# Trainium2, one core: expert products collected by half features, memory splits spread over the convolution, GpSimd emptied in the second block, the norm folded into cos and sin

## The chip, the core and the metric

The kernel runs on one core of a Trainium2 chip. A core has a matrix engine (PE, with its weight loads shown as PEld), three engines for elementwise work (DVE, ACT, POOL) and a queue of DMA issues on SP. Each engine takes its instructions in the order in which the program was scheduled, and waits on semaphores for the others. The metric is device time of one execution in microseconds, lower is better.

## The reference

256 tokens of width 1024 pass a first block (modulated norms, retention and differential attention, then a mixture of 16384 single-neuron experts) and a second block of two layers. Cut to what the change touches:

```
x = x + mod[:, 5] * peer_ffn(h2, ...)              # end of the first block
# second block, layer 0                               (rms_norm before each h)
b_gate, c_gate, u = split(h @ conv_w_in, 3)
x = x + (b_gate * conv3(c_gate * u)) @ conv_w_out   # 3 taps along the tokens
x = x + mem_cross_attention(h, mem_n, ...)          # keys and values of 256 memory tokens
x = x + swiglu(h)
# layer 1
k, v = split(rms_norm(x, kv_norm) @ w_kv, 2);  k = apply_partial_rope(k, cos, sin)
q = apply_partial_rope(h @ moba_w_q, cos, sin)
x = x + causal_softmax(q k^T * 128**-0.5) v @ moba_w_o
x = x + mem_cross_attention(...);  x = x + swiglu(h);  out = rms_norm(x, g)
```

## The kernel before

**Layout and products.** Activations lie as [128 features, chunk k of 8, 256 tokens]. A product of a 128x1024 weight block with an activation is `block`: the raw block is loaded by DMA (three buffers, `raw`), ACT rounds it to `whi`, DVE or POOL subtracts to `wlo` (`split_w`, L121, two `wlo` buffers), and PE does 24 products of 128x128 by 128x256: eight chunks k each of whi·xh, wlo·xh and whi·xl (`mm3`, L143). With `late=True` the 24 run chunk by chunk, so that the first block can begin before all of x is there. The activation's own halves come from `gain_chunk`: `hh` on ACT, `hl` on DVE (L269, L270).

**Order.** A scheduler orders each engine's instructions when the program is built. By hand come two things. `PLACES` names the points (`at(...)`) where steps of a *filler* are put: one step is one 24-product block of the keys and values of the second memory attention (tiles `fill`, `hmh`, `hml`, `memk1`, `memv1`), which depends on nothing near it. And `lo_plan` and the argument `lo` say which engine makes a block's `wlo`; `FILL_LO = 'p'` puts that of the filler on POOL.

**The seam between the blocks.** Experts go in 128 chunks; chunk products of 128x512 (L948) add into four banks `acc[th][dh]` (token half, feature half). The last two chunks are done for token half 0, then 1; `collect(th)` copies four quarters out of PSUM (L956), transposes eight 128x128 tiles on PE (L961) and adds each into x with the gate (L964).

**Convolution** (`conv_mixer`). For each of eight output chunks m, PE does the blocks of c_gate, u (tile `o`) and b_gate (tile `b`). The norm's r is needed only afterwards: squares of x are summed in `track` (ACT squares, `self.adder` adds, L225), one product with ones makes the sum (`aux`), and `rstd` makes r (`nry`). `gate` then works off chunk m: cu = o·r (DVE), z (POOL), first tap (DVE), two taps (DVE), y·r (POOL), ct = b·y (DVE, L1246, reads PSUM), ch (ACT), cl (DVE). Chunk 0 is gated only when chunk 1 has been computed, so `b` of chunk 0 holds its PSUM bank until `ct` of chunk 0 is made. At m = 1, `hook()` loads the first memory attention's keys and values from DRAM (tile `kvt`, two buffers) and splits them: `memk0h`, `memv0h` on ACT, `memk0l`, `memv0l` on POOL (L1086).

**Moba layer.** w_v, then eight heads of w_k and of moba_wq. `plain` takes each out of PSUM with scale and r (`qkt`, L1373); `rope_out` shuffles (DVE), multiplies with cos (POOL, L384) and with sin (DVE, L385) and adds (DVE, L386).

Of the kernel before, what the change touches and what calls it, by code (L numbers as in the profile page):

```python
# [25 lines left out]
P = 128  # L26
# [14 lines left out]
PLACES = {0: 1, 3: 1, 5: 2, 6: 1, 10: 1, 12: 1, 's': 2, 'h': 4, 'g': 10, 'n': 1, ('g', 0): 1, 'v': 4, ('d', 1): 1, ('o', 0): 3, ('o', 2): 1, ('o', 3): 1, ('o', 4): 1, ('o', 5): 4, ('o', 7): 10, ('c', 1): 1, ('c', 3): 1, ('c', 5): 1, 'ce': 1, 'm0': 1, 'mq0': 1, 'me0': 1, 'f0': 1, 'b': 2, 'bk': 1, 'bq': 1, ('mh0', 2): 1, ('bh', 0): 1, ('bh', 5): 1, ('bh', 7): 1}  # L41
# [7 lines left out]
HOOK = 1  # L49
# [6 lines left out]
CADD = 'vector'  # L56
# [14 lines left out]
class Build:  # L71
    def __init__(self, ctx, tc, io):
        self.ctx, self.tc, self.nc, self.io = ctx, tc, tc.nc, io
        self.const = ctx.enter_context(tc.tile_pool(name="const", bufs=1))
        self.wpool = ctx.enter_context(tc.tile_pool(name="weights", bufs=2))
        self.psfill = ctx.enter_context(tc.tile_pool(name="psfill", bufs=1, space=PSUM))
        self.lo_turn = 0
        self.folding = []
        self.filler = self.steady = iter(())
        self.rate, self.due = RATE, 0  # L80
        self.adder = self.nc.gpsimd
        self.lo_plan = "v"
# [356 lines left out]
    def mixer(self):  # L439
        nc, io, tc = self.nc, self.io, self.tc  # L440
        with ExitStack() as ctx:
# [7 lines left out]
            with ExitStack() as c1:  # L449
# [18 lines left out]
                self.adder = nc.vector  # L468
# [235 lines left out]
    def peer(self):  # L704
        nc, io = self.nc, self.io
        with ExitStack() as ctx:
# [237 lines left out]
            def product(c, th, a, b, w):  # L944
                tsl = slice(th * P, th * P + P)
                for s, (x, wt) in enumerate(((a, w[0]), (b, w[0]), (a, w[1]))):
                    for dh in range(2):
                        nc.tensor.matmul(acc[th][:, dh], x[:, tsl], wt[:, dh * 512:dh * 512 + 512],  # L948
                                         start=c == 0 and s == 0, stop=c == NCH - 1 and s == 2)

            def collect(th):

                tsl = slice(th * P, th * P + P)
                for q in range(4):
                    e = nc.scalar.copy if th or q % 2 else nc.vector.tensor_copy
                    e(ot[:, th, q * T:(q + 1) * T], acc[th][:, q // 2, q % 2 * T:q % 2 * T + T])  # L956
                for q in range(2):
                    tr = self.psum([P, 4, P])
                    for i in range(4):
                        k = 4 * q + i  # L960
                        nc.tensor.transpose(tr[:, i], ot[:, th, k * P:(k + 1) * P], self.ident)  # L961
                    for i in range(4):
                        k = 4 * q + i
                        nc.vector.scalar_tensor_tensor(self.x[:, k, tsl], tr[:, i], gate[:, k:k + 1],  # L964
                                                       self.x[:, k, tsl], op0=OP.mult, op1=OP.add)
# [12 lines left out]
            for c, parts in ends:  # L978
                product(c, 0, *parts)
            product(ends[0][0], 1, *ends[0][1])  # L980
            collect(0)
            product(ends[1][0], 1, *ends[1][1])
            collect(1)


    def mem_kv(self, pool, mpool, l, key, value, norm=None):
# [38 lines left out]
        yield from self.natural_steps("fill", [io["mem_wv"][l, q] for q in range(8)], toks,  # L1025
                                      lambda n, i, o: value(n, o, rn), FILL_LO)
# [47 lines left out]
    def mem_load(self, pool, l):  # L1074
# [3 lines left out]
        def load():  # L1078
            for n in range(4):
                for part in range(2):  # L1080
# [5 lines left out]
                    nc.gpsimd.tensor_sub(lo, t, hi)  # L1086

        return (kT, v), load

    def mem_fill(self, pool, mpool, l):  # L1090
# [3 lines left out]
        def key(n, o, r):  # L1094
# [4 lines left out]
            nc.gpsimd.tensor_sub(lo, t, hi)  # L1099
# [125 lines left out]
    def conv_mixer(self, hook):  # L1225
        nc, io = self.nc, self.io
        with ExitStack() as ctx:
# [5 lines left out]
            def gate(m, o, b):  # L1233
                cu = pool.tile([P, 2, T], F32, name="cu", tag="cu", bufs=2)
                nc.vector.tensor_mul(cu, o, r[:, None, :].to_broadcast([P, 2, T]))
                z = pool.tile([P, T], F32, name="z", tag="z", bufs=2)
                nc.gpsimd.tensor_mul(z, cu[:, 0], cu[:, 1])
                y = pool.tile([P, T], F32, name="cy", tag="cy", bufs=2)
                nc.vector.tensor_scalar(y, z, cw[:, m, 2:3], None, op0=OP.mult)
# [4 lines left out]
                nc.gpsimd.tensor_mul(y, y, r)  # L1244
# [5 lines left out]
            self.adder = getattr(nc, CADD)  # L1250
            for k in range(KC):
                self.track(self.x[:, k], k)
            self.adder = nc.gpsimd
            for m in range(KC):
                self.at(("c", m))
                if m == HOOK:
                    hook()
                o = self.psum([P, 2, T], "sc" if m < 2 else "mm")
                for i, c in enumerate((1, 2)):
                    self.block(o[:, i], io["conv_wi"][8 * c + m], h, late=m == i == 0)  # L1260
                    if m == 1 and i == NORM1:
                        r = self.tracked_norm(pool, "nr", tables=True)
                b = self.psum([P, T])
# [78 lines left out]
    def moba(self):  # L1342
        nc, io = self.nc, self.io
        with ExitStack() as ctx:
            pool = self.pool(ctx, "moba")
            mask = self.load(pool, "causal", [P, 2, T])
            hk = self.gained(pool, self.x, G_KV)
            v = pool.tile([P, 2, 1024], F32, name="v")
# [5 lines left out]
            def value(n, i, o):  # L1354
# [3 lines left out]
                if n == 1:  # L1358
                    rn = self.by_partition(pool, r, "aux")
                waiting.append((n, o))  # L1360
# [8 lines left out]
            def plain(block, h, scale):  # L1369
                o = self.psum([P, T])  # L1370
                self.block(o, block, h)
                t = pool.tile([P, T], F32, name="qkt", tag="qkt", bufs=3)
                nc.vector.scalar_tensor_tensor(t, o, scale, r, op0=OP.mult, op1=OP.mult)  # L1373
                return t

            def rope(out, t):
                self.rope_out(pool, t, out, self.pcos, self.psin)
# [4 lines left out]
            hq = [self.placed(pool, "hq" + c, 32) for c in "hl"]  # L1382

            def query(hd):
                return plain(io["moba_wq"][hd], hq, 128.0 ** -0.5)
# [5 lines left out]
            for hd in range(KC):  # L1391
                t = plain(io["w_k"][hd], hk, 1.0)
# [3 lines left out]
                self.gain_chunk(self.x[:, hd], G_MIX + 1, hd, hq[0][:, hd], hq[1][:, hd])  # L1396
# [224 lines left out]
```

## Time and profile before

| | |
|---|---|
| median of 3 runs | 1904.57 us (1903.88 to 1911.25) |
| profiled execution | 1898.9 us, of it the span of the trace 1897.0 us |
| mean granted TensorE clock | 0.984 |
| busy: PE, DVE, ACT, POOL | 1830.2, 1324.2, 968.1, 541.2 us |
| last expert product, start | 1127.17 us into the span |
| convolution, first product to last | 1132 to 1255 us, about |
| moba layer | 1505 to 1630 us, about |
| second memory attention, second swiglu | 1633 to 1700, 1704 to 1885 us, about |

Times are microseconds from the span's start. Some 60% of the span lies ahead of the seam and is the same code in both kernels; the change acts from about 1125 us on.

### The profile page before, as it was taken

The page shows a single profiled execution, that of the slowest core. Times are in us where ns is not written, and L with a number is a line of the kernel's source. Part 1 is how long each engine was busy: PE and PEld are TensorE (multiplying, and loading weights), DVE is VectorE, ACT ScalarE, POOL GpSimd, SP SyncE. Part 2 cuts the span into 40 slices and gives each one's busy share as a digit, 9 for nine tenths or more (in the row PEclk, how much of TensorE's full clock was granted, in tenths as well). Part 3 has the DMA queues.
Part 4 walks back from the last instruction along what each step waited for, and adds up shares of the span by engine and source line. Part 5 has one row for each costly group of instructions (what it writes and reads, how often), then busy time and mean ns, then how long its engine had stood idle before and what let it go on. Part 6 is the DMA issues. An engine that isn't in the chain of part 4 may idle for free.

```text
span 1897.0 us, 34717 instructions
## 1 busy us (share of the span) xinstructions
PE 1830.2 (96%) x13488; PEld 1713.1 (90%) x13488; DVE 1324.2 (70%) x2594; ACT 968.1 (51%) x1517; POOL 541.2 (29%) x289
## 2 busy tenths in 40 slices
PE   5899999999999999999999998999999999999997
PEld 4696788999999999788888878999999998999997
DVE  8988965995556676865555568677765678766654
ACT  5645534545554444454545454455554545555543
POOL 2511115787776767100000004242000222110001
PEclk8999999999999999999999998999999999999999
DMA  7673435555444444765656565654666553545553
GB/s 265 222 244 101 133 123 169 172 194 170 163 152 157 155 160 152 251 190 190 198 190 195 192 201 168 190 165 152 197 195 195 188 177 120 167 133 183 187 188 123
DMA packets 99765, 335.13 MB, mean 177 GB/s; under 512 B 12400, under 2 KB 13456, under 8 KB 99216
## 3 DMA queue, kind: packets, MB, share of 16 engines
q1 hardware_dynamic: 98160, 330.68, 53.4%
q8 instruction: 106, 1.74, 0.4%
q10 hardware_dynamic: 1440, 2.23, 0.3%
q14 instruction: 59, 0.48, 0.1%
HBM read 329.59 MB, written 3.28 MB: 175 GB/s over the span
## 4 chain that ended last, share of the span: by engine, by line
PE 86%; DVE 8%; ACT 2%; issue 2%; DMA 1%; POOL 1%; SPq 0%; DVEq 0%; ACTq 0%; POOLq 0%
PE mm L143 53%; PE pair L948 18%; PE mm L178 4%; PE pair L885 3%; PE fill L178 1%; PE fill L143 1%; DVE wlo L121 1%; PE sc L143 1%; PE aux L143 1%; ACT whi L117 1%; DMA mraw<-w_mod 0%; PE sc L546 0%; POOL wlo L121 0%; DMA raw<-w_mod 0%; DVE macc L361 0%
## 5 line engine op out<-in xcount | busy, mean ns | idle before, releaser
L117 ACT CAST whi<-raw 128x1024 fp32r<-128x1024 f32 x564 | 591.8, 1051 | 548.8 <-PE mm L143 261.6
L121 DVE TENSOR_TENSOR wlo<-raw,whi 128x1024 fp32r<-128x1024 f32 x389 | 489.1, 1259 | 277.9 <-PE pair L948 130.7
L121 POOL TENSOR_TENSOR wlo<-raw,whi 128x1024 fp32r<-128x1024 f32 x175 | 425.2, 2431 | 276.3 <-PE mm L143 169.2
L143 PE MATMUL mm<-hh,whi 128*128 128x256 f32 (+1 forms) x1184 | 177.6, 287 | 6.5 <-DVE ct L1246 5.0
L225 POOL TENSOR_TENSOR acc<-acc,accsq 128x256 f32<-128x256 f32 x42 | 42.6, 1015 | 491.3 <-ACT accsq L223 491.3
L143 PE MATMUL mm<-hl,whi 128*128 128x256 f32 (+1 forms) x1184 | 174.4, 285 | 0.9 <-DVE hl L270 0.9
L143 PE MATMUL mm<-hh,wlo 128*128 128x256 f32 (+1 forms) x1184 | 173.5, 285 | 0.6 <-DVE wlo L121 0.6
L143 PE MATMUL mm<-h2h,whi 128*128 128x256 f32 x1152 | 166.9, 287 | 4.1 <-ACT h2h L255 4.0
L143 PEld LDWEIGHTS mm<-hh,whi 128*128 128x128 f32 x1184 | 154.4, 190 | 12.0 <-issue 7.4
L948 PE MATMUL pair<-whi,actl 128*128 128x512 f32 x512 | 159.0, 392 | 1.8 <-DVE actl L941 1.8
L948 PE MATMUL pair<-whi,acth 128*128 128x512 f32 x512 | 158.7, 391 | 0.4 <-ACT acth L940 0.4
L948 PE MATMUL pair<-wlo,acth 128*128 128x512 f32 x512 | 158.4, 391 | 0.3 <-DVE wlo L121 0.3
L143 PEld LDWEIGHTS mm<-hh,wlo 128*128 128x128 f32 x1184 | 153.4, 189 | 4.3 <-issue 1.5
L143 PEld LDWEIGHTS mm<-hl,whi 128*128 128x128 f32 x1184 | 153.5, 189 | 3.5 <-DVE hl L270 1.6
L143 PE MATMUL mm<-h2l,whi 128*128 128x256 f32 x1152 | 156.1, 278 | 0.0
L143 PE MATMUL mm<-h2h,wlo 128*128 128x256 f32 x1152 | 156.0, 278 | 0.0
L143 PEld LDWEIGHTS mm<-h2h,whi 128*128 128x128 f32 x1152 | 146.3, 191 | 5.0 <-ACT h2h L255 4.8
L143 PEld LDWEIGHTS mm<-h2l,whi 128*128 128x128 f32 x1152 | 143.1, 188 | 0.0
L143 PEld LDWEIGHTS mm<-h2h,wlo 128*128 128x128 f32 x1152 | 143.0, 188 | 0.0
L948 PEld LDWEIGHTS pair<-whi,actl 128*128 128x128 f32 x512 | 95.9, 188 | 23.1 <-DVE actl L941 3.2
L948 PEld LDWEIGHTS pair<-wlo,acth 128*128 128x128 f32 x512 | 96.6, 189 | 20.9 <-DVE wlo L121 0.7
L948 PEld LDWEIGHTS pair<-whi,acth 128*128 128x128 f32 x512 | 96.0, 188 | 20.7 <-ACT acth L940 1.0
(408 smaller groups left out, 3111.5 us busy)
## 6 DMA issues: line engine op xcount, KB each, us to landing
raw<-peer_u SPq DMA_DIRECT2D x128, 512.0 KB, 3.5
raw<-peer_v SPq DMA_DIRECT2D x128, 512.0 KB, 3.5
raw<-ffn_gu SPq DMA_DIRECT2D x88, 512.0 KB, 3.9
raw<-ffn_dn SPq DMA_DIRECT2D x44, 512.0 KB, 3.5
raw<-w_mod SPq DMA_DIRECT2D x64, 256.0 KB, 3.8
raw<-conv_wi SPq DMA_DIRECT2D x24, 512.0 KB, 3.6
raw<-mem_wk SPq DMA_DIRECT2D x16, 512.0 KB, 5.2
mraw<-w_mod SPq DMA_DIRECT2D x16, 512.0 KB, 6.2
```

The costliest lines, as they stand in the source:

```text
L117: self.hi_copy = nc.scalar.copy(hi, raw)
L121: (nc.vector if plan == "v" else nc.gpsimd).tensor_sub(lo, raw, hi)
L143: self.matmul = nc.tensor.matmul(out, a, b, start=first and j == 0, stop=last and j == 3 * n - 1)
L178: self.matmul = nc.tensor.matmul(outs[i // 2][:, i % 2], a[:, k, :], b[:, w], start=k == 0 and s == 0 and i % 2 == 0, stop=k == 7 and s == ...
L225: self.adder.tensor_add(self.acc, self.acc, self.last)
L885: nc.tensor.matmul(o[:, 2 * j + i], A[:, i], Bt[:, i], start=True, stop=True)
L948: nc.tensor.matmul(acc[th][:, dh], x[:, tsl], wt[:, dh * 512:dh * 512 + 512], start=c == 0 and s == 0, stop=c == NCH - 1 and s == 2)
```

## The change

Six edits. (1) The last two chunks' products and `collect` go by feature half dh, with th inside; each `collect(th, dh)` has one ACT copy, one DVE copy, four transposes and four additions. (2) `late` takes a number: the convolution's first block does chunks 0 to 3 in all three products, then 4 to 7. (3) `mem_load` is a generator; two of its eight steps are drawn for each m from 3 on, instead of all at m = 1, and its subtractions, those of the second memory's loads and the `wlo` of the filler are on DVE. (4) Two filler steps no longer stand at m = 1 and m = 3; they are left to the `fill(20)` ahead of the second memory attention. (5) `self.adder` is DVE in the second block, `gate` has its two POOL multiplications on DVE (z = o0·r², then z·o1, both from PSUM), and its first tap is on ACT. (6) In the moba layer r is multiplied into cos and sin once (`cosr`, `sinr`), the scale of q into its gains, and `rope` reads the product in PSUM directly with four DVE instructions.

```diff
-PLACES = {..., ('c', 1): 1, ('c', 3): 1, ('c', 5): 1, ...}
+PLACES = {..., ('c', 5): 1, ...}
-HOOK = 1
+HOOK = 3
-        self.adder = self.nc.gpsimd
+        self.adder = self.nc.vector
...
-            order.sort(key=lambda si: (si[1], si[0]))
+            order.sort(key=lambda si: (si[1] // int(late), si[0], si[1]))
...
-            def collect(th):
+            def collect(th, dh):
...
+                for q, e in zip((2 * dh, 2 * dh + 1), (nc.scalar.copy, nc.vector.tensor_copy)):
+                    e(ot[:, th, q * T:(q + 1) * T], acc[th][:, dh, q % 2 * T:q % 2 * T + T])
...
-            for c, parts in ends:
-                product(c, 0, *parts)
-            product(ends[0][0], 1, *ends[0][1])
-            collect(0)
-            product(ends[1][0], 1, *ends[1][1])
-            collect(1)
+            waiting = None
+            for dh in range(2):
+                for th in range(2):
+                    for c, parts in ends:
+                        product(c, th, *parts, halves=(dh,))
+                    if waiting:
+                        collect(*waiting)
+                    waiting = th, dh
+            collect(*waiting)
...
-                self.block(o[:, i], io["mem_wk"][l, 2 * m2 + i], hm, lo=FILL_LO, late=m2 == i == 0,
+                self.block(o[:, i], io["mem_wk"][l, 2 * m2 + i], hm, lo="v" if l else FILL_LO, late=m2 == i == 0,
...
-                    nc.gpsimd.tensor_sub(lo, t, hi)
+                    nc.vector.tensor_sub(lo, t, hi)
+                    yield
...
-                cu = pool.tile([P, 2, T], F32, name="cu", tag="cu", bufs=2)
-                nc.vector.tensor_mul(cu, o, r[:, None, :].to_broadcast([P, 2, T]))
-                nc.gpsimd.tensor_mul(z, cu[:, 0], cu[:, 1])
+                nc.vector.tensor_mul(z, o[:, 0], r2)
+                nc.vector.tensor_mul(z, o[:, 1], z)
-                nc.vector.tensor_scalar(y, z, cw[:, m, 2:3], None, op0=OP.mult)
+                nc.scalar.activation(y, z, AF.Copy, scale=cw[:, m, 2:3])
...
-                nc.gpsimd.tensor_mul(y, y, r)
+                nc.vector.tensor_mul(y, y, r)
...
-                if m == HOOK:
-                    hook()
+                if m >= HOOK:
+                    for _ in range(2):
+                        next(hook, None)
...
+                    nc.vector.tensor_mul(cosr, self.pcos, r)
+                    nc.vector.tensor_mul(sinr, self.psin, r)
...
+            def rope(out, o):
+                t = pool.tile([P, T], F32, name="roper", tag="roper", bufs=2)
+                nc.vector.stream_shuffle(t, o, [(i + 16) % 32 for i in range(32)])
+                nc.vector.tensor_mul(out, o, cosr)
+                nc.vector.tensor_mul(t, t, sinr)
+                nc.vector.tensor_add(out, out, t)
                 return out
```

How the scheduler's order moves is shown at three places; line numbers of the changed kernel are one or two lower for the same code. First DVE at the seam, before: the quarter copies out of PSUM (`slots<-pair`), two splits of convolution weights (`wlo`), the additions into x, then `hl` for the convolution.

```order
L956 COPY slots<-pair 128x256 x2
L121 TENSOR_TENSOR wlo<-raw,whi 128x1024
L964 SCALAR_TENSOR_TENSOR x<-mm,mod,x 128x128 x8
L121 TENSOR_TENSOR wlo<-raw,whi 128x1024
L964 SCALAR_TENSOR_TENSOR x<-mm,mod,x 128x128 x8
L270 SCALAR_TENSOR_TENSOR hl<-x,gains,hh 128x256 x8
L225 TENSOR_TENSOR acc<-acc,accsq 128x256
L121 TENSOR_TENSOR wlo<-raw,whi 128x1024
```

The same place on DVE in the changed kernel:

```order
L953 COPY slots<-pair 128x256 x2
L960 SCALAR_TENSOR_TENSOR x<-mm,mod,x 128x128 x8
L953 COPY slots<-pair 128x256
L120 TENSOR_TENSOR wlo<-raw,whi 128x1024
L960 SCALAR_TENSOR_TENSOR x<-mm,mod,x 128x128 x4
L953 COPY slots<-pair 128x256
L120 TENSOR_TENSOR wlo<-raw,whi 128x1024
L960 SCALAR_TENSOR_TENSOR x<-mm,mod,x 128x128 x4
L269 SCALAR_TENSOR_TENSOR hl<-x,gains,hh 128x256 x8
L224 TENSOR_TENSOR acc<-acc,accsq 128x256
L120 TENSOR_TENSOR wlo<-raw,whi 128x1024
L224 TENSOR_TENSOR acc<-acc,accsq 128x256
```

One copy and one split now stand between the last two groups of additions, and all eight `hl` still come after the last addition.

Second, POOL from the first memory split to the third gated chunk, before (in the changed kernel POOL has nothing between the last expert chunk and the final norm):

```order
L1086 TENSOR_TENSOR memk0l<-kvt,memk0h 128x512
L1086 TENSOR_TENSOR memv0l<-kvt,memv0h 128x2x256
L1237 TENSOR_TENSOR z<-cu 128x256
L1086 TENSOR_TENSOR memk0l<-kvt,memk0h 128x512
L1237 TENSOR_TENSOR z<-cu 128x256
L1086 TENSOR_TENSOR memv0l<-kvt,memv0h 128x2x256
L1244 TENSOR_TENSOR cy<-cy,nry 128x256
L121 TENSOR_TENSOR wlo<-raw,whi 128x1024
L1244 TENSOR_TENSOR cy<-cy,nry 128x256
```

And DVE of the changed kernel from the norm's last step (`nry`) to `ct` of the first two chunks:

```order
L211 SCALAR_TENSOR_TENSOR nry<-nra,nry 128x256
L120 TENSOR_TENSOR wlo<-raw,whi 128x1024
L1263 TENSOR_TENSOR r_12403<-nry 128x256
L269 SCALAR_TENSOR_TENSOR hml<-memx,gains,hmh 128x256
L1235 TENSOR_TENSOR z<-sc,r_12403 128x256 x2
L1236 TENSOR_TENSOR z<-sc,z 128x256 x2
L120 TENSOR_TENSOR wlo<-raw,whi 128x1024
L1239 SCALAR_TENSOR_TENSOR cy<-z,conv_w,cy 128x255 x2
L1241 SCALAR_TENSOR_TENSOR cy<-z,conv_w,cy 128x254 x2
L1243 TENSOR_TENSOR cy<-cy,nry 128x256 x2
L1245 TENSOR_TENSOR ct<-mm,cy 128x256 x2
```

Between the end of the `hl` and the first `ct` DVE holds seven `wlo`, four of the eight memory splits, eight additions to `acc`, seven `hml`, the norm and the gating of two chunks; the other four memory splits come after it.

Third, DVE in the moba layer where the first two filler blocks stand, before, from the rope of the last head of k to that of the second head of q:

```order
L386 TENSOR_TENSOR k<-k,roper 128x256
L1373 SCALAR_TENSOR_TENSOR qkt<-mm,nry 128x256
L383 STREAM_SHUFFLE roper<-qkt 128x256
L385 TENSOR_TENSOR roper<-roper,psin 128x256
L386 TENSOR_TENSOR q<-q,roper 128x256
L121 TENSOR_TENSOR wlo<-raw,whi 128x1024
L1373 SCALAR_TENSOR_TENSOR qkt<-mm,nry 128x256
```

The same place in the changed kernel:

```order
L1388 TENSOR_TENSOR k<-k,roper 128x256
L120 TENSOR_TENSOR wlo<-raw,whi 128x1024
L1385 STREAM_SHUFFLE roper<-mm 128x256
L1386 TENSOR_TENSOR q<-mm,cosr 128x256
L1387 TENSOR_TENSOR roper<-roper,sinr 128x256
L1388 TENSOR_TENSOR q<-q,roper 128x256
L120 TENSOR_TENSOR wlo<-raw,whi 128x1024
L1385 STREAM_SHUFFLE roper<-mm 128x256
```

Before, the `wlo` of these two filler blocks are on POOL; the first `wlo` in this piece is now that of the first filler block.

## Rows read from the trace of the kernel before

**Rows 1.** The page, part 4: shares of the chain that ended last.
```profile
PE 86%; DVE 8%; ACT 2%; issue 2%; DMA 1%; POOL 1%; SPq 0%; DVEq 0%; ACTq 0%; POOLq 0%
```

**Rows 2.** Stretches: length, busy PE, PEld, DVE, ACT, POOL (count), granted clock, DMA share.
```profile
1136.00:1166.00 30.00, 23.41 (x176) 22.63 (x175) 26.44 (x30) 17.02 (x28) 16.48 (x11) 0.89 0.61 194
1166.00:1180.00 14.00, 12.13 (x84) 12.16 (x85) 10.44 (x16) 5.23 (x7) 5.58 (x5) 0.76 0.34 107
1180.00:1255.00 75.00, 74.39 (x646) 74.02 (x646) 51.99 (x72) 37.31 (x50) 26.72 (x22) 1.00 0.59 190
```

**Rows 3.** PE from 1127 to 1174: start, length, instruction, count [idle before, releaser].
```profile
1127.17 0.62 PE L948 MATMUL pair<-wlo,acth 128*128 128x512 f32 x2
...
1132.11 0.55 PE L143 MATMUL sc<-hh,whi 128*128 128x256 f32 x1 [2.07 <-ACT hh L269]
...
1136.95 1.07 PE L143 MATMUL sc<-hh,whi 128*128 128x256 f32 x8
...
1146.79 2.07 PE L143 MATMUL sc<-hh,wlo 128*128 128x256 f32 x8 [3.27 <-DVE wlo L121]
...
1161.82 1.07 PE L143 MATMUL mm<-hl,whi 128*128 128x256 f32 x8
1167.87 2.04 PE L143 MATMUL mm<-hh,whi 128*128 128x256 f32 x8 [4.98 <-DVE ct L1246]
...
1173.08 0.28 PE L143 MATMUL fill<-hmh,whi 128*128 128x256 f32 x1
```

**Rows 4.** DVE from 1131 to 1172, columns as in the rows above.
```profile
1131.93 3.24 DVE L270 SCALAR_TENSOR_TENSOR hl<-x,gains,hh 128x256 fp32r<-128x256 f32 x8
...
1139.86 0.48 DVE L270 SCALAR_TENSOR_TENSOR hml<-memx,gains,hmh 128x256 fp32r<-128x256 f32 x1
1140.26 0.42 DVE L225 TENSOR_TENSOR acc<-acc,accsq 128x256 f32<-128x256 f32 x1
1140.60 1.52 DVE L270 SCALAR_TENSOR_TENSOR hml<-memx,gains,hmh 128x256 fp32r<-128x256 f32 x1
...
1145.53 5.65 DVE L121 TENSOR_TENSOR wlo<-raw,whi 128x1024 fp32r<-128x1024 f32 x3
...
1158.53 1.22 DVE L121 TENSOR_TENSOR wlo<-raw,whi 128x1024 fp32r<-128x1024 f32 x1
...
1167.30 0.42 DVE L1246 TENSOR_TENSOR ct<-mm,cy 128x256 f32<-128x256 f32 x1 [0.61 <-POOL cy L1244]
...
1171.17 0.68 DVE L1235 TENSOR_TENSOR cu<-mm,nry 128x512 f32<-128x512 f32 x1
```

**Rows 5.** POOL at the first memory split.
```profile
1140.26 1.58 POOL L1086 TENSOR_TENSOR memk0l<-kvt,memk0h 128x512 fp32r<-128x512 f32 x1 [370.24 <-ACT memk0h L1085]
```

**Rows 6.** PE in the moba layer, the two filler blocks that wait.
```profile
1560.04 0.38 PE L178 MATMUL fill<-wlo,hmh 128*128 128x256 f32 x1 [1.13 <-POOL wlo L121]
...
1569.55 0.55 PE L178 MATMUL fill<-whi,hmh 128*128 128x256 f32 x1 [3.23 <-DVE bsst L1123]
...
1572.43 0.28 PE L178 MATMUL fill<-whi,hml 128*128 128x256 f32 x1
```

**Rows 7.** DVE in the moba layer, an addition that ends a rope, and the filler's value.
```profile
1557.85 2.41 DVE L386 TENSOR_TENSOR k<-k,roper 128x256 f32<-128x256 f32 x1
...
1568.54 0.87 DVE L1105 SCALAR_TENSOR_TENSOR memv1l<-fill,memrn,memv1h 128x256 fp32r<-128x256 f32 x2
```

**Rows 8.** POOL in the moba layer, the filler's first split.
```profile
1557.42 2.56 POOL L121 TENSOR_TENSOR wlo<-raw,whi 128x1024 fp32r<-128x1024 f32 x1
```

**Rows 9.** Waits of PE after 1110: releaser, us in total, times, longest.
```profile
PE mm L143 <- DVE hl L270: 0.9, 3, 0.5
...
PE mm L143 <- ACT ch L1247: 0.6, 1, 0.6
```

**Rows 10.** The chain in order of time, the two longest pieces: start, us, what.
```profile
1324.95 174.11 PE mm L143 x1536
...
1704.27 180.92 PE mm L143 x1536
```

More of the change, by code (lines that the diff above doesn't have):

```diff
@@ L55 @@
 BYP = 2
-CADD = 'vector'
 MIXLO = 'v'
@@ L942, in chunk, with product @@
                 return a, b, w
-            def product(c, th, a, b, w):
+            def product(c, th, a, b, w, halves=range(2)):
                 tsl = slice(th * P, th * P + P)
                 for s, (x, wt) in enumerate(((a, w[0]), (b, w[0]), (a, w[1]))):
-                    for dh in range(2):
+                    for dh in halves:
                         nc.tensor.matmul(acc[th][:, dh], x[:, tsl], wt[:, dh * 512:dh * 512 + 512],
                                          start=c == 0 and s == 0, stop=c == NCH - 1 and s == 2)
-            def collect(th):
+            def collect(th, dh):
                 tsl = slice(th * P, th * P + P)
[L954 to L965, printed above, removed]
+                for q, e in zip((2 * dh, 2 * dh + 1), (nc.scalar.copy, nc.vector.tensor_copy)):
+                    e(ot[:, th, q * T:(q + 1) * T], acc[th][:, dh, q % 2 * T:q % 2 * T + T])
+                tr = self.psum([P, 4, P])
+                for i in range(4):
+                    k = 4 * dh + i
+                    nc.tensor.transpose(tr[:, i], ot[:, th, k * P:(k + 1) * P], self.ident)
+                for i in range(4):
+                    k = 4 * dh + i
+                    nc.vector.scalar_tensor_tensor(self.x[:, k, tsl], tr[:, i], gate[:, k:k + 1],
+                                                   self.x[:, k, tsl], op0=OP.mult, op1=OP.add)
             gate = self.mod[:, 40:48, 0]
@@ L1248, in gate @@
                 nc.vector.tensor_sub(cat[1][:, m], t, cat[0][:, m])
-            self.adder = getattr(nc, CADD)
+            self.adder = nc.vector
             for k in range(KC):
                 self.track(self.x[:, k], k)
-            self.adder = nc.gpsimd
             for m in range(KC):
                 self.at(("c", m))
-                if m == HOOK:
-                    hook()
+                if m >= HOOK:
+                    for _ in range(2):
+                        next(hook, None)
                 o = self.psum([P, 2, T], "sc" if m < 2 else "mm")
                 for i, c in enumerate((1, 2)):
-                    self.block(o[:, i], io["conv_wi"][8 * c + m], h, late=m == i == 0)
+                    self.block(o[:, i], io["conv_wi"][8 * c + m], h, late=4 if m == i == 0 else 0)
                     if m == 1 and i == NORM1:
                         r = self.tracked_norm(pool, "nr", tables=True)
+                        r2 = pool.tile([P, T], F32, name="r2")
+                        nc.vector.tensor_mul(r2, r, r)
                 b = self.psum([P, T])
@@ L1347, in moba @@
             hk = self.gained(pool, self.x, G_KV)
+            nc.vector.tensor_scalar(self.gains[:, G_MIX + 1], self.gains[:, G_MIX + 1], 128.0 ** -0.5, None,
+                                    op0=OP.mult)
+            hq = [self.placed(pool, "hq" + c, 40) for c in "hl"]
+            cosr, sinr = (pool.tile([P, T], F32, name=n) for n in ("cosr", "sinr"))
             v = pool.tile([P, 2, 1024], F32, name="v")
@@ L1359, in value @@
                     rn = self.by_partition(pool, r, "aux")
+                    nc.vector.tensor_mul(cosr, self.pcos, r)
+                    nc.vector.tensor_mul(sinr, self.psin, r)
+                for k in (2 * n, 2 * n + 1):
+                    self.gain_chunk(self.x[:, k], G_MIX + 1, k, hq[0][:, k], hq[1][:, k])
                 waiting.append((n, o))
@@ L1367, in moba, with plain @@
             self.natural("mm", [io["w_v"][q] for q in range(8)], toks, value)
-            def plain(block, h, scale):
+            def plain(block, h):
                 o = self.psum([P, T])
                 self.block(o, block, h)
[L1372 to L1377, printed above, removed]
+                return o
+            def rope(out, o):
[4 more added lines that the diff above has]
+                nc.vector.tensor_add(out, out, t)
                 return out
@@ L1381, in moba @@
             kT = pool.tile([P, KC, T], F32, name="k")
-            hq = [self.placed(pool, "hq" + c, 32) for c in "hl"]
             def query(hd):
-                return plain(io["moba_wq"][hd], hq, 128.0 ** -0.5)
+                return plain(io["moba_wq"][hd], hq)
             def turned(t):
```

12 lines of the change are left out of this document (5 added, 7 removed).

## The prediction

> **What bounds the kernel now.** I read the chain of waits first. PE holds 86% of it and DVE 8% [rows 1], so a change off PE can only pay where PE stands still or runs at the lower granted clock. Next the table of stretches after the seam. From 1180 on the convolution is full of PE: 74.39 busy of 75 us at a granted clock of 1.00. Ahead of that it is not: 23.41 of 30 us at 0.89, then 12.13 of 14 us at 0.76 [rows 2]. The timeline of PE says where. The first product of the convolution waits 2.07 us, a block in chunk 1 waits 3.27 us for a `wlo` of DVE, and the `b` block of chunk 2 waits 4.98 us for `ct` of chunk 0, which frees its PSUM bank [rows 3]. From 1167.87 to 1173.08 that block's 24 products take 5.21 us [rows 3]; at the rate of the first swiglu (174.11 us for 1536 products, 0.1133 each) they take 2.72 [rows 10]. So a wait costs about 2.5 us more than itself, the time at the lower level of the clock, 1.2 GHz instead of 2.4, that follows it.
>
> Why is DVE late there? Between 1136 and 1166 it is busy 26.44 of 30 us beside POOL's 16.48 [rows 2], but many of its instructions are stretched. `hml` takes 0.48 us, and 1.52 once it starts at 1140.60, while POOL's `memk0l` runs from 1140.26 for 1.58 [rows 4, 5]; three `wlo` take 5.65 us where three single ones take 3 x 1.22 = 3.66 [rows 4]. The moba layer shows the same: the addition at 1557.85 takes 2.41 us beside a `wlo` on POOL that runs from 1557.42 for 2.56 [rows 7, 8], where an addition of that size takes 0.42 [rows 4]. PE then waits 1.13 us for that POOL split and 3.23 us for a PSUM bank of the filler, whose reader `memv1l` stands behind the late ropes on DVE at 1568.54 [rows 6, 7].
>
> The Trainium skill ("SBUF — State Buffer", section Who interferes with whom) says that a DVE instruction with two SBUF inputs and a GpSimd instruction that reads SBUF exclude each other for a whole instruction. The rows agree: the 1.52 us `hml` ends 0.28 us after `memk0l`. The page's practical rule, that the one to issue second blocks until the first finishes, would make every POOL operation beside DVE cost its full length, and by it the gain of the convolution would lie at the upper end given below.
>
> **The change part by part.** *Seam.* Before, the last expert product ends at 1127.17 + 0.62 = 1127.79; I call this t0. The `hl` run from t0+4.14 to t0+7.38 [rows 4], and the 28 products ahead of 1136.95 are done at t0+9.16 [rows 3]. In the new order the eight `hl` still stand behind the last addition, and that behind, in turn, four additions, a copy and a split. Half of eight additions is about 1.1 us (an `hl`, 0.40 each, is a larger one), the copy 0.4 and the split 1.2, then four more additions 1.1, with hops: `hl` begins at about t0+5 and ends at t0+8.35, 1 us later. Against this the `hh` of chunks 0 to 3 are ready while the last products run, so PE needs only the last few products after the last `hl`: 28 done at t0+8.6 to t0+9.2. I take 0, with bounds of -1 and +1 us.
>
> *Convolution.* Two POOL multiplications a chunk and eight memory splits go to DVE. Their price there: the split of 128x512 has the size of `cu`, 0.68 us; the others are of 128x256, 0.42 [rows 4]. The two stretched pieces above alone give back 1.04 and 1.99 us. So DVE's work up to the first `ct`, by the new order after the last `hl`, each counted from start to next start (some 0.08 us less than its length): eight `acc` at 0.33 are 2.7 us, seven `wlo` at 1.14 are 8.0, four splits at 0.61 are 2.4, seven `hml` at 0.40 are 2.8, four steps of the norm 1.8, r2 0.35, four `z` 1.4, four taps 1.7, two multiplications by r 0.8 and `ct` 0.4: together 22.4 us, hence t0+8.35+22.4 = t0+30.7. Before, `ct` ended at 1167.30 + 0.42, t0+39.9 [rows 4]. PE meanwhile has, after its 28 products, 164 more to the same place (20 left of the first `b`, six blocks of 24): 164 x 0.1133 = 18.6 us, so it arrives at about t0+27.5 and still waits some 3 us, no longer 4.98, and the 3.27 us wait in chunk 1 and its slow time are swallowed. After the wait I leave the slow 5.21 us as it was. Gain 39.9 - 30.7 = 9.2 us. Upper bound: DVE ahead of PE, no wait and no slow time, 39.9 - 27.5 + 2.5 = 15. Lower bound: DVE also waits for ACT's first tap, for `whi` and for `wlo` buffers that PE frees; 6 us of that leaves 3. I take 9.
>
> From chunk 2 on a chunk has 72 products, 8.16 us. DVE then does three `wlo` (3.4 us), `z` twice, two taps, y·r, `ct`, `cl` (seven at about 0.4, 2.8 us), in all 6.2, with two memory splits 7.4. That lies under PE, and no gain is left there but the 0.6 us for `ch` [rows 9]. The two filler steps only move; their 48 products cost the same elsewhere.
>
> *Second layer.* `wlo` of the filler at 1.22 us on DVE costs its queue less than the 2.0 us by which a POOL split stretched the addition. In the new order the first filler's `wlo` stands ahead of the first rope of q, so the 1.13 us go; `memv1l` comes about one split and two additions behind its product, so of the 3.23 I leave 0.6; the slow time after it (13 products took 1572.43 - 1569.55 = 2.88 us until the clock came back, for 1.5 at full rate [rows 6]) goes too, 1.3. Sum 5.1; I take 4.5, bounds 2 and 5.7. If the cover of PE's queue were gone, the four rope instructions, now reading PSUM and holding the bank longer, would cost up to 0.4 each for ten heads, 4 us; PE's own 2.72 us a head hides all but the last. *Second memory attention.* Two more filler blocks stand ahead of it and cover `hl`: 0.9 us [rows 9]; I take 0.7, bounds 0 and 2. The sums on DVE instead of POOL (0.42 each, some 35) lie under PE's products: 0.
>
> **Sum.** 0 + 9.0 + 0.5 + 4.5 + 0.7 = 14.7 us. The profiled execution took 1898.9 us (1897.0 of span and 1.9 around it), 5.7 under the median; I subtract from either: 1884.2 beside the profile, 1904.6 - 14.7 = 1889.9 as a median. Bounds of the terms together: 1 lost at the seam, 3, 0, 2, 0 is 4; 1, 15, 0.6, 5.7, 2 is 24. The time is 1880 to 1901 by these.
>
> **The rivals.** A measurement of this kernel can tell about 0.5%, 9.5 us: faster is below 1895.0, slower above 1914.1.
>
> *A, forecast:* gain 10 to 20, about 1890.
>
> *B, DVE becomes the bound of the convolution's start.* For it speaks that DVE was 88% busy there [rows 2] and takes on all of POOL's work in strict order; against it, that much of these 88% is stretch. At 6 us of waits the gain is 3 + 5.7 = 8.7, no measurable change, 1896. The Trainium skill ("Perfetto Trace Analysis", section Optimizing Scalar/DVE Operations) would rather take work off a full DVE, even to GpSimd, but adds that the shared port may spoil this; the rows show that it does here.
>
> *C, the rate of PE changes with the new order.* The same 1536 products of a swiglu take 174.11 us in layer 0 and 180.92 in layer 1 [rows 10], both at granted clock 1.00, with nothing waited for: 0.1133 against 0.1178 a product. I found no cause in the rows. If the first layer (about 390 us at the faster rate) falls to the slower one, 390 x 0.04 = 15.6 us are lost and the gain is gone, 1905, no change; for the first swiglu alone 6.8, 1897. If the second swiglu rises instead, 6.8 more are won, 1883.
>
> *D, the other side: DVE above 8.16 us in every chunk of the convolution.* Each `gate` now has two round trips to ACT (first tap, `ch`) with `wlo` queued behind. Were each exposed at 2 us, a chunk would take 7.4 + 4 = 11.4 us of DVE, 3.2 above PE, over six chunks 19 us, plus about half as much in lower clock as after the waits above, 28 in all: 1890 + 28 = 1918, slower. It begins to cost at 0.8 us of exposed waiting a chunk, and makes the kernel slower by over 0.5% from about 3.5. Against it: `cl` stands after other work in the new order, and first taps come in pairs.
>
> *E, the stalls were not the bound,* and another wait (weights' DMA) takes their place: about 1901. PE is 0.99 busy right after 1180 with a DMA share of 0.59, beside 0.61 before [rows 2], which speaks against it.
>
> **Chances.** A 0.50, C upward (1878 to 1885) 0.14, B 0.12, C downward 0.12, E 0.05, D 0.07. The likeliest gives 1890; its own range is 1884 to 1895. Leaving out D and the tails of C, 1879 to 1905. Below 1895: A almost whole, C upward, a little of B and C downward, 0.66; slower is D, 0.07; the rest, 0.27, the same.
>
> **What would show it.** Right: no POOL row after the seam but the last, `hml` at 0.48 throughout, the `ct` wait at about t0+27.5 of some 3 us and none for `wlo` before it, 1.13 and 3.23 us gone in the moba layer, the convolution's last product some 9 us earlier against t0 plus the moved filler's 5.7. Wrong: `hl` ending later than t0+9, a DVE wait in every chunk, a swiglu of layer 0 near 181 us.

## The result, and the profile after

The changed kernel takes 1892.76 us (median of 16 runs, 1887.35 to 1899.19) beside 1905.54 of the kernel before (16 runs, 1897.81 to 1912.35). The ratio on record is 0.9938, 95% interval 0.9921 to 0.9954: faster by 0.62%, which is 11.8 us, between 8.8 and 15.1; the two medians lie 12.8 us apart. Forecast were 1890 us, 14.7 us faster, and a range of 1879 to 1905. Two repetitions of the changed kernel gave 0.9928 (0.9909 to 0.9947) and 0.9932 (0.9905 to 0.9958). The profiled execution took 1892.6 us, 1890.7 of it span.

What PE waits for after the seam, by the list of waits (releaser, us in total, times, longest; only those over 1 us). The 3.3 and 5.0 us of the convolution and both waits of the moba layer are gone or smaller; 2.7 us for `memv1l` are new:

```profile
PE fill L177 <- DVE memv1l L1105: 2.7, 1, 2.7
PE sc L142 <- ACT hh L268: 1.8, 1, 1.8
PE mm L142 <- DVE ct L1245: 1.7, 1, 1.7
PE mm L957 <- DVE slots L953: 1.5, 1, 1.5
```

PE at the seam and the start of the convolution, from the first of the last 24 expert products to the block after the `ct` wait (to be read beside [rows 3]):

```profile
1126.31 0.39 PE L946 MATMUL pair<-whi,acth 128*128 128x512 f32 x1
...
1133.07 0.39 PE L946 MATMUL pair<-wlo,acth 128*128 128x512 f32 x1
...
1138.38 0.71 PE L142 MATMUL sc<-hh,whi 128*128 128x256 f32 x4 [1.82 <-ACT hh L268]
...
1143.29 1.07 PE L142 MATMUL sc<-hh,whi 128*128 128x256 f32 x8
...
1161.80 1.10 PE L142 MATMUL mm<-hl,whi 128*128 128x256 f32 x8
1164.60 1.15 PE L142 MATMUL mm<-hh,whi 128*128 128x256 f32 x8 [1.70 <-DVE ct L1245]
...
1167.41 1.07 PE L142 MATMUL mm<-hh,whi 128*128 128x256 f32 x8
```

t0, the end of the last expert product, is 1133.07 + 0.39 = 1133.46. The 28th product is done at 1143.29, t0+9.8 (before t0+9.2); the waiting block starts at t0+31.1 (before 1167.87, t0+40.1); and its 24 products take 1167.41 - 1164.60 = 2.81 us at a granted clock of 1.00, not 5.21. DVE over the same stretch:

```profile
1138.15 3.24 DVE L269 SCALAR_TENSOR_TENSOR hl<-x,gains,hh 128x256 fp32r<-128x256 f32 x8
...
1144.34 0.68 DVE L1085 TENSOR_TENSOR memk0l<-kvt,memk0h 128x512 fp32r<-128x512 f32 x1
...
1149.60 0.48 DVE L269 SCALAR_TENSOR_TENSOR hml<-memx,gains,hmh 128x256 fp32r<-128x256 f32 x1
...
1164.04 0.75 DVE L1245 TENSOR_TENSOR ct<-mm,cy 128x256 f32<-128x256 f32 x2
```

`hml` takes 0.48 us and a memory split 0.68. The first `ct` ends at 1164.04 + 0.41 = 1164.45, t0+31.0; forecast was t0+30.7. By stretches (busy PE, PEld, DVE, ACT, POOL, granted clock, as in [rows 2]), POOL has nothing left, DVE is busy 0.98 of the time until the waiting block and 0.96 in the 15 us after it, with PE full at the clock of 1.00:

```profile
1143.29:1164.60 21.31, 19.61 (x168) 19.38 (x167) 20.79 (x41) 18.10 (x32) 0.00 (x0) 1.00 0.80 256
1164.60:1180.00 15.40, 15.40 (x136) 15.40 (x137) 14.85 (x26) 8.27 (x12) 0.00 (x0) 1.00 0.63 206
```

**The stages of all profiles.** One execution's total mixes the change with the rate of PE (next section), so I compare stages between rows that both kernels have: from the first of the last 24 expert products to the first swiglu's 1536 products, these products, and from their end to those of the second swiglu. For before that is 1324.95 - 1121.09, 174.11, and 1704.27 - 1499.06 [rows 10], with this row of before:

```profile
1121.09 0.61 PE L948 MATMUL pair<-whi,acth 128*128 128x512 f32 x2
```

All stages are in us. A star marks kernels in which 48 filler products are done after the first stage instead of in it (5.7 us, two blocks of 2.86).

| kernel | seam to swiglu 1 | swiglu 1 | to swiglu 2 | ratio to before, 95% interval |
|---|---|---|---|---|
| before | 203.9 | 174.1 | 205.2 | |
| before, again | 203.3 | 180.9 | 205.4 | |
| changed * | 185.3 | 180.9 | 205.5 | 0.9938, 0.9921 to 0.9954 |
| changed, again * | 185.0 | 180.9 | 208.3 | 0.9928, 0.9909 to 0.9947 |
| changed, third * | 185.3 | 180.9 | 206.0 | 0.9932, 0.9905 to 0.9958 |
| splits on DVE alone | 197.1 | 180.9 | 205.3 | 0.9959, 0.9937 to 0.9981 |
| spreading alone | 199.6 | 180.9 | 205.1 | 0.9992, 0.9975 to 1.0009 |
| splits, spreading and moba | 199.6 | 180.9 | 200.0 | 0.9916, 0.9886 to 0.9945 |
| moba alone | 204.0 | 180.9 | 198.9 | 0.9987, 0.9975 to 0.9999 |
| filler's splits on DVE alone | 203.0 | 180.9 | 201.2 | 0.9963, 0.9945 to 0.9982 |
| changed, seam as before * | 186.3 | 180.9 | 206.4 | 0.9947, 0.9926 to 0.9967 |
| changed, gating on POOL * | 189.4 | 180.9 | 207.0 | 0.9956, 0.9937 to 0.9976 |
| changed, filler in the heads * | 188.9 | 180.9 | 204.0 | 0.9922, 0.9898 to 0.9946 |
| the same again * | 187.1 | 180.9 | 204.4 | 0.9917, 0.9892 to 0.9942 |

By the means of the profiles, and with the 5.7 us set right, the change gives 203.6 - (185.2 + 5.7) = 12.7 us in the first stage and 205.3 - (206.6 - 5.7) = 4.4 in the second, 17.1 in all. PE has two rates inside these stages too. Counted by the distance from one product's start to the next (0.113 or 0.118 us), 366 and 445 products of the first stage are at the slower rate in before's two profiles, and 376, 378 and 373 in the changed kernel's; in the second stage 883 and 635 beside 608, 806 and 762. In the means that is some 0.3 of the 17.1 us; between single profiles it can be 1 to 2 us.

### The profile page after: what moved, and what is told of

It reads as the page before. It is cut to its first block, busy times and chain, and to the rows that moved or that the text cites. A ratio compares the mean times of both kernels' runs of the same rounds, so it can differ in the third digit from the quotient of the medians.

```text
span 1890.7 us, 34567 instructions
## 1 busy us (share of the span) xinstructions
PE 1829.8 (97%) x13488; PEld 1715.8 (91%) x13488; DVE 1337.7 (71%) x2678; ACT 970.1 (51%) x1523; POOL 413.1 (22%) x187
## 4 chain that ended last, share of the span: by engine, by line
PE 87%; DVE 7%; ACT 2%; DMA 2%; issue 1%; POOL 0%; SPq 0%; DVEq 0%; ACTq 0%; POOLq 0%
PE mm L142 55%; PE pair L946 17%; PE mm L177 4%; PE pair L883 3%; PE fill L177 2%; PE fill L142 2%; PE sc L142 1%; DMA raw<-peer_v 1%; DVE wlo L120 1%; PE aux L142 1%; DMA kvt<-kv 0%; DMA raw<-w_mod 0%; DVE mlo L120 0%; POOL wlo L120 0%; ACT whi L116 0%
## 5 line engine op out<-in xcount | busy, mean ns | idle before, releaser
L120 DVE TENSOR_TENSOR wlo<-raw,whi 128x1024 fp32r<-128x1024 f32 x405 | 496.6, 1227 | 261.5 <-PE pair L946 130.7
L120 POOL TENSOR_TENSOR wlo<-raw,whi 128x1024 fp32r<-128x1024 f32 x159 | 386.1, 2429 | 228.1 <-PE mm L142 157.9
```

What stands on the lines that cost most here:

```text
L120: (nc.vector if plan == "v" else nc.gpsimd).tensor_sub(lo, raw, hi)
```

## The experiments

**The rates of PE.** Both kernels once more, unedited, and the changed one a third time.

> The changed kernel once more. Theory A (the two rates of PE, 0.1133 and 0.1178 us a product of 128x256, fall out anew in each execution): the first swiglu's 1536 products, 180.9 us in the first profile, can come out at 174 as well, and the 767 products of the experts' query stage, which no edit touches (90.3 us there, 87.0 before), change too. Theory B (the change's new order sets the rate): the first swiglu stays at 181 and the query stage at 90. Both: the time about 1892 and the stretch from the end of the expert products to the third chunk's b block of the convolution the same as in the first profile within 0.5 us.

> The kernel before once more, for its rates. Theory A: the first swiglu (174.1 us in the first profile) or the second (180.9) or the query stage (87.0) comes out otherwise. Theory B: 174.1, 180.9 and 87.0 again. Both: the waits of PE in the convolution as before, 3.3 us for the weight split and 5.0 us for ct.

The chain's longest pieces, first of the changed kernel, then of its repetition, then of before's repetition and of the kernel with the spreading alone (start, us, what):

```profile
359.55 90.34 PE mm L142 x767
...
1311.64 180.91 PE mm L142 x1536
...
1698.01 180.92 PE mm L142 x1536
```

```profile
360.73 86.95 PE mm L142 x767
```

```profile
359.92 86.95 PE mm L143 x767
...
1326.94 180.92 PE mm L143 x1536
```

```profile
1323.11 180.91 PE mm L143 x1536
...
1709.13 174.12 PE mm L143 x1536
```

The query stage, the same instructions in all kernels, takes 86.95 or 90.34 us for 767 products, and the repetition of the changed kernel has the other value than its first profile. Before's first swiglu is 174.11 once and 180.92 once. Theory A: the rate falls out anew in each execution. It is not the chip alone: of the profiles taken on one chip, both repetitions have 86.95 and the splits on DVE alone have 90.34. Over 14 profiles the first swiglu was fast once (before) and the second once (spreading alone). So 174.11 in the profile from which I predicted was an exception, and a single profile pair cannot tell a change of 7 us.

> The changed kernel a third time, to compare with on the same chip. If the lower clock after the wait for ct is the chip's choice and not the kernel's, its 24 products there take anything from 2.8 to 5.2 us; if the shorter wait of 1.7 us is what avoids it, 2.8 to 3.3 again. The wait for memv1l 2.7 us again; the first swiglu 181 or 174 us.

It came as the first two: the `ct` wait 1.67 us with 24 products in 2.82 behind it, the `memv1l` wait 2.72 us, the first swiglu at 180.91.

**Splits on DVE alone.**

```diff
-                    nc.gpsimd.tensor_sub(lo, t, hi)
+                    nc.vector.tensor_sub(lo, t, hi)
```

> The kernel before with one edit: the eight subtractions of the first memory's keys and values on DVE instead of POOL; still all drawn at chunk 1, z and y times r still on POOL. Theory A (POOL's long splits stretch DVE's instructions, and that made the convolution late): no DVE instruction of 128x1024 over 1.3 us between the seam and the first ct except beside z, the 3.3 us wait gone, ct of chunk 0 some 6 us earlier, about 6 us faster in all. Theory B (the amount of DVE work before ct is what counts, the splits must be spread out): the eight splits add 5 us to DVE's queue before ct, so the wait for ct stays or grows, no gain, time within 2 us of before.

The 3.3 us wait for DVE's `wlo` is gone, the stage is 6.5 us shorter and the kernel 0.41% faster: theory A, with more DVE work and less time. But `ct` came only 2.3 us earlier (t0+37.6) and not 6, because the remaining POOL work still met DVE ahead of it. DVE's split, then POOL's, then what PE waits for:

```profile
1159.98 2.82 DVE L1086 TENSOR_TENSOR memv0l<-kvt,memv0h 128x512 fp32r<-128x512 f32 x1
```

```profile
1159.47 2.79 POOL L121 TENSOR_TENSOR wlo<-raw,whi 128x1024 fp32r<-128x1024 f32 x1
```

```profile
1162.31 0.58 PE L143 MATMUL fill<-hmh,wlo 128*128 128x256 f32 x1 [3.41 <-POOL wlo L121]
```

The split that alone takes 0.68 us takes 2.82, from 1159.98 to 0.54 us after the POOL split ended (1159.47 + 2.79 = 1162.26). The Trainium skill ("SBUF — State Buffer", section Who interferes with whom) calls the contention of two such instructions an exclusive lock, in which the order of issue decides who blocks. The trace agrees: had the split waited for POOL's end and then taken its 0.68 us, it would have ended 0.14 us later than it did.

**Spreading alone.** `load` as a generator, two steps for each m from 3 on, still on POOL.

> The kernel before with the spreading alone: two of the first memory's eight loads drawn for each chunk from 3 on, their subtractions still on POOL. Theory A (what counts is that POOL's splits run beside DVE): they run somewhat later, still ahead of the first ct since they depend on nothing there, and stretch DVE as before; the wait for ct stays at 4 to 6 us, the stretch from seam to first swiglu within 2 us of before's 196 to 197 us. Theory B (the spreading makes the gain): the two waits, 3.3 and 5.0 us, shrink to under 3 together, and the stretch is 6 us or more shorter.

In between: the `ct` wait shrank to 2.99 us, the stage by 4.0, and the time not measurably. Five of the eight splits started on POOL ahead of the first `ct` all the same, where all eight did before. They stretched DVE less: the three `wlo` that took 5.65 us [rows 4] took 4.67.

**Gating back on POOL.**

```diff
-                nc.vector.tensor_mul(z, o[:, 0], r2)
-                nc.vector.tensor_mul(z, o[:, 1], z)
+                nc.vector.tensor_mul(cu, o, r[:, None, :].to_broadcast([P, 2, T]))
+                nc.gpsimd.tensor_mul(z, cu[:, 0], cu[:, 1])
...
-                nc.vector.tensor_mul(y, y, r)
+                nc.gpsimd.tensor_mul(y, y, r)
```

> The changed kernel with the gating's multiplications z and y times r back on POOL (cu on DVE again); the splits stay on DVE. Theory A (the long POOL splits did the harm, short POOL operations of 0.75 us little): the ct wait grows by the two hops through POOL, from 1.7 to about 3 us, with some slow time after it; 1 to 3 us slower than the changed kernel in the convolution. Theory B (any POOL work beside DVE costs its length): sixteen operations of 0.75 us, 12 us, of which the convolution's slack hides half; 5 us slower or more.

The stage is 4.2 us longer than the changed kernel's, by the figure between the theories. But not all of it is POOL's. The `ct` wait is no longer (1.44 us); new is one wait of 1.32 us in the last chunk, whose gate now goes through POOL twice:

```profile
1215.63 0.38 PE L142 MATMUL mm<-ch,whi 128*128 128x256 f32 x1 [1.32 <-ACT ch L1247]
```

Some 1.5 us are PE's slower rate, in 703 products of the stage instead of 373 to 378, and 0.9 stand already at the block behind the `ct` wait, which starts 39.0 us after the first of the 24 expert products instead of 37.9 to 38.3. What the wait itself adds is of theory A's size: short POOL operations do little harm in this profile.

**The seam as before, the rest changed.**

> The changed kernel with the last two chunks' products and collect by token halves as before. Theory A (the seam by feature halves costs, as the two profiles read: 7.1 instead of 6.7 us for the products and 4.9 instead of 4.4 to the first product of the convolution): the stretch from the first of the last 24 expert products to the first product of the convolution is 11.0 us instead of 12.1, and the ct wait grows by no more than 0.5; the kernel 1 us faster than the changed one. Theory B (the hh of the first four chunks, ready earlier, pay this back): the stretch to the third chunk's b block is the same as in the changed kernel or longer.

The stretch to the first product of the convolution is 11.1 us instead of 12.1, as A said. The block behind the `ct` wait starts 37.7 us after the first of the 24 expert products instead of 37.9 to 38.3, so most of that microsecond is paid back by there, as B said, but not all. The first swiglu then begins no earlier (186.3 beside 185.0 to 185.3). What goes lost behind the `ct` wait is the clock:

```profile
1161.15 1.34 PE L142 MATMUL mm<-hh,whi 128*128 128x256 f32 x8 [1.79 <-DVE ct L1244]
...
1165.58 1.07 PE L142 MATMUL mm<-hh,whi 128*128 128x256 f32 x8
```

24 products take 4.43 us at a granted clock of 0.60 after a wait of 1.79, where the changed kernel's take 2.81 at 1.00 after 1.70. Since the clock fell after such a wait in one profile of the new seam too (below), this one profile cannot tell which seam is better.

**The moba layer: rope alone, and the filler's splits alone.**

> The kernel before with the moba edits alone (norm in cos and sin, rope from PSUM on DVE alone; the filler's weight splits still on POOL). Theory A (the filler's splits on POOL stretch DVE's instructions, whoever does the multiplication with cos): the filler's first block still waits about 1 us, a rope instruction beside a POOL split still takes over 2 us, and the wait for the filler's bank stays at 2 to 3 us; gain of the kernel under 2 us. Theory B (POOL's multiplication in the rope was what held DVE): the two waits shrink to under 1 us together and the kernel gains 3 to 5 us.

> The kernel before with the filler's weight splits on DVE alone; rope still with POOL's multiplication, first memory's splits still on POOL. Theory A (the long POOL split made the two waits of the moba layer): both waits, 1.1 and 3.2 us, go to under 1 together. Theory B (DVE needs 3.1 us a head of k, more than PE's 2.72, because POOL's multiplication stretches rope, and is late there whoever splits the filler): DVE still takes 3.1 us a head and is late by as much; the first wait is for DVE's split and the sum of waits stays above 3 us; the second layer gains under 2 us.

Successive heads on DVE, first with the moba edits alone, then with the filler's splits on DVE alone:

```profile
1562.60 0.46 DVE L1384 STREAM_SHUFFLE roper<-mm 128x256 f32<-128x256 f32 x1
...
1563.26 0.41 DVE L1386 TENSOR_TENSOR roper<-roper,sinr 128x256 f32<-128x256 f32 x1
...
1565.32 0.46 DVE L1384 STREAM_SHUFFLE roper<-mm 128x256 f32<-128x256 f32 x1
```

```profile
1558.61 0.42 DVE L1373 SCALAR_TENSOR_TENSOR qkt<-mm,nry 128x256 f32<-128x256 f32 x1
...
1559.07 0.45 DVE L383 STREAM_SHUFFLE roper<-qkt 128x256 f32<-128x256 f32 x1
1559.55 0.58 DVE L385 TENSOR_TENSOR roper<-roper,psin 128x256 f32<-128x256 f32 x1
...
1562.17 0.45 DVE L383 STREAM_SHUFFLE roper<-qkt 128x256 f32<-128x256 f32 x1
```

A head goes by on DVE in 2.72 us with the moba edits and in 3.10 without them, as before. PE's own head is 2.72, so before, DVE fell 0.38 us behind in each head, and this delay reached PE in the two waits. Beside POOL's multiplication the one with sin takes 0.58 us instead of 0.41; the rest of the 0.38 came with the other moves of the edit (`qkt` goes from DVE, the multiplication with cos comes to it), which no run takes apart. So that POOL's multiplication was the cause, as theory B of both runs has it, is shown in part only. With the moba edits both waits are gone though the filler's `wlo` is still on POOL, and the stage is 6.4 us shorter. The whole time shows less, 0.13% (0.01 to 0.25). With the filler's splits alone the waits shrink from 4.4 to 1.9 us together and the stage by 4.1, between the theories of that run:

```profile
1568.06 0.39 PE L178 MATMUL fill<-wlo,hmh 128*128 128x256 f32 x1 [0.58 <-DVE wlo L121]
...
1575.66 0.36 PE L178 MATMUL fill<-whi,hmh 128*128 128x256 f32 x1 [1.31 <-DVE memv1l L1105]
```

So either edit removes much of the wait, by different ways, and their gains do not add up.

**Two edits together.** Splits on DVE and spread, and moba; seam, gating, sums and filler as before.

> The kernel before with two of the six edits: the first memory's splits on DVE and drawn from chunk 3 on, and the moba layer's rope and norm. Seam, gating, sums, filler and its places as before. Theory A (these two carry the change): seam to first swiglu 194 to 196 us instead of 203.5 from the first of the last 24 expert products, the first swiglu's end to the second's start 199 instead of 205.3, the kernel 12 to 15 us faster than before, as fast as the changed one within 3 us. Theory B (the POOL operations of the gating and the two moved filler blocks are needed): seam to first swiglu stays above 198, the kernel 5 to 9 us faster than before.

The profile is with B (199.6 and 200.0 us, 9.3 us gained), the timing with A (0.9916), with an interval of 0.6%, too wide to decide. So whether the other four edits add anything to these two is not shown by timing; in the profiles they add 7.8 us, about 1 of which is PE's slower rate in the first stage here. In the profile a filler split on POOL takes the place of the old wait, and a granted clock of 0.50 follows, from 1167.1 to 1172.3:

```profile
1164.11 0.39 PE L143 MATMUL fill<-hmh,wlo 128*128 128x256 f32 x1 [2.57 <-POOL wlo L121]
...
1167.09 2.08 PE L143 MATMUL mm<-hh,whi 128*128 128x256 f32 x8 [1.64 <-DVE ct L1247]
```

**The new wait ahead of the second memory attention.** In the changed kernel, the second of three filler blocks there, on PE, and then what stands ahead of `memv1l` on DVE:

```profile
1619.71 0.28 PE L177 MATMUL fill<-wlo,hmh 128*128 128x256 f32 x1
1622.72 0.36 PE L177 MATMUL fill<-whi,hmh 128*128 128x256 f32 x1 [2.73 <-DVE memv1l L1105]
...
1627.53 0.28 PE L177 MATMUL fill<-whi,hmh 128*128 128x256 f32 x1
```

```profile
1618.97 1.28 DVE L269 SCALAR_TENSOR_TENSOR hl<-x,gains,hh 128x256 fp32r<-128x256 f32 x3
1620.17 1.22 DVE L120 TENSOR_TENSOR wlo<-raw,whi 128x1024 fp32r<-128x1024 f32 x1
1621.30 0.48 DVE L269 SCALAR_TENSOR_TENSOR hl<-x,gains,hh 128x256 fp32r<-128x256 f32 x1
1621.70 0.87 DVE L1105 SCALAR_TENSOR_TENSOR memv1l<-fill,memrn,memv1h 128x256 fp32r<-128x256 f32 x2
```

The block's PSUM bank is read by `memv1l`, and that waits behind four `hl` and a weight split. After 2.73 us of waiting PE falls to the lower clock at about 1624 (granted clock 0.51 from 1624.0 to 1627.5): from 1622.72 to 1627.53, 4.81 us for 27 products that take 3.1 at 0.1133. The edit puts two of the blocks into the heads:

```diff
-('bh', 0): 1, ('bh', 5): 1, ('bh', 7): 1}
+('bh', 0): 1, ('bh', 2): 1, ('bh', 4): 1, ('bh', 5): 1, ('bh', 7): 1}
```

> The changed kernel with two of the three filler blocks ahead of the second memory attention moved into the moba heads 2 and 4. Theory A (the new wait of 2.7 us there is the filler's single PSUM bank, whose reader memv1l stands behind hl and a weight split on DVE; with one block left there is no second one to wait): the wait and the 1.7 us of slow clock behind it go, no new wait over 0.6 us in the heads, 3 to 4 us faster than the changed kernel from the first swiglu's end to the second's start. Theory B (three blocks cover hl there, and DVE is full in the heads): the wait for hl ahead of the attention comes back at 2 us or more, or the heads wait for their splits, and the time is the same.

> The changed kernel with two filler blocks in moba heads 2 and 4, once more, beside the changed kernel on the same chip. Theory A (the wait for the filler's bank ahead of the second memory attention costs its 2.7 us and some slow clock): first swiglu's end to second's start 202 to 204 us, no wait for memv1l, median 2 to 4 us under that of the changed kernel. Theory B (the heads pay for it): 206 us or more and the same median.

Theory A, with a smaller gain than its 3 to 4 us: no wait for `memv1l`, none over 0.6 us in the heads, the stage 204.0 and 204.4 us instead of 205.5 to 208.3, 2.4 less in the mean. Part of it goes to 1.3 us of waiting for `qh` inside the attention (0.5 to 1.0 before, none in the changed kernel). The medians, 1889.74 and 1890.53, lie 1.4 to 3 us under those of the changed kernel, 1891.89 to 1892.76; the intervals overlap, so a better version is likely, not shown by timing. Its first stage was longer, 188.9 and 187.1 us, on code that is the same there: in one profile 0.9 us went in the expert products, 1.2 to 1.5 in the convolution's first 28 products and some 1.7 in PE's slower rate (754 products instead of 373 to 378), in the other the clock after the `ct` wait fell again (24 products in 4.22 us after a wait of 1.76).

## Why the prediction held, and where its steps were off

The direction, the place and nearly the size were right: 11.8 us measured, 14.7 forecast. That the total came so close is partly luck, since the terms missed both ways. Step by step:

*Seam: 0, bounds -1 and +1.* `hl` ended at 1138.15 + 3.24 = t0+7.9, 0.4 us sooner than worked out. But the sentence that the `hh` of chunks 0 to 3 would be ready while the last products run was wrong: ACT had its eight `hh` in one piece, after the last transposes, and PE waited 1.82 us for them. From the first of the 24 products to the 28th of the convolution it is 1143.29 - 1126.31 = 17.0 us instead of 15.9, a loss of 1.1. By the run with the old seam all but 0.2 to 0.6 us of it is gone at the block behind the `ct` wait; whether that rest is lost for good stays open.

*Convolution: 9.* The mechanism is shown: stretched DVE instructions were the delay, and they are back at their own lengths. `ct` at t0+31.0 beside t0+30.7, PE's block 8.9 us earlier, forecast 9.2. The wait was 1.70 us and not some 3, but not because DVE was quicker: PE came later, at t0+29.4 instead of t0+27.5, its 28 products 0.9 us later than taken and 94 of the 163 after them at the slower rate, 0.4 us. Mis-sized was "After the wait I leave the slow 5.21 us as it was": after this shorter wait the clock stayed up, 2.4 us more gain in all three profiles of the changed kernel. Only the upper bound of the forecast held this, and it is partly luck, as the profile with 4.22 us shows. The rest of the stage, up to 12.7, I did not follow to single waits; 0.6 of it is the `ch` wait [rows 9]. Rival B's 6 us of waits did not come, but DVE is near to bounding PE: 0.98 busy up to the block, 0.96 after it.

*Second layer: 4.5.* 119.3 us on average from the first w_v product to the last of moba_wo, beside 125.0: 5.7 gained, the upper bound. The named cause, the filler's split, was only part of it; the rate of a head on DVE, 3.10 against 2.72 us, was the other, and to set that right was alone enough.

*Second memory attention: 0.7.* This failed. The added filler blocks do cover `hl`, but the second needs the bank of the first, and the memory value that frees it stands behind the very `hl` that it was to cover. The stretch from moba_wo's end to the second swiglu rose from 74.7 us (mean of two) to 81.7 (of three), 1.2 more than the 5.7 that moved there.

*Sum.* The stages give 17.1 us, the three ratios 11.8 to 13.7. For the profiles the difference is accounted for: their spans are 1901.5 us before and 1889.4 changed in the mean, 12.1 apart. 3.4 us of the 17.1 go because before had one fast first swiglu in two profiles and the changed kernel none in three; 1.7 go ahead of the seam, where the code is the same (the first of the 24 products starts at 1122.4 us before and 1124.1 changed, in the mean). That the runs without a profile lose it the same way is not shown. Rival C was real as a price (6.8 us) but wrong as a mechanism: before's repetition has the slow first swiglu too, so the new order does not set the rate. For the same reason the swiglu of layer 0 near 181 us, which the prediction names as a sign of being wrong, came in all three profiles and was no such sign.

## What to carry to other kernels

Where the instructions of one engine stretch those of another, cost a move by what it does to the other's instructions: read the same operation's length with and without a neighbour, and sum the excess. A filler in front of a stall helps only if what frees its buffer isn't queued behind that stall. And compare stages between rows that both kernels have, over several profiles, and count what PE's rate makes of them, before a few microseconds of one profile are called a gain.

## What was not expected of the hardware

PE ran the same 1536 products in 174.1 or 180.9 us, and the same 767 in 86.95 or 90.34, at granted clock 1.00 and with nothing waited for, differing between executions of one program. A wait of 1.64 to 1.70 us left the granted clock at 1.00 in three profiles of the changed kernel, while after waits of 1.76 and 1.79 us 24 products took 4.2 and 4.4 us. No rule follows from that: with two edits alone it was low after 1.64 us too, but there a wait of 2.57 us had ended 1.3 us before.
